# First modulation vectors from w_ada blocks as the stationary operand, first tiles transposed between them

## Chip, cores and metric

The kernel runs on one core of one Trainium2 chip. The metric is device time in microseconds (us); of the kernel before, three runs took 2872.82, 2876.39 and 2877.79 us, median 2876.39.

## What is computed

One layer of a diffusion trunk: an HGRN2 mixer (gated linear recurrence, both directions) and a gated ConvFFN over 2048 latent tokens of width 1024, with 256 context tokens as a prefix. The change is in what comes first, the adaLN modulation:

```python
sc_lat, sc_ctx = jax.nn.silu(c), jax.nn.silu(c_ctx)
m_l = (sc_lat @ w_ada[l] + b_ada[l])[:, None, :]
m_c = sc_ctx @ w_ada[l] + b_ada[l]
sh1, sc1, g1, sh2, sc2, g2 = jnp.split(m_l, 6, axis=-1)
csh1, csc1, cg1, csh2, csc2, cg2 = jnp.split(m_c, 6, axis=-1)
hl = modulate(rmsnorm(lat, norm_g[l, 0]), sh1, sc1)
hc = modulate(rmsnorm(cx, norm_g[l, 0]), csh1, csc1)
```

`modulate(h, shift, scale)` is `h * (1 + scale) + shift`. w_ada is 1024 x 6144 in float32; the first 2048 of its columns give the shift and the scale of the mixer, for two vectors, latent and context.

## The kernel before

Five engines run in order, each through its own list, and wait for each other by semaphores: PE (matrix products), PEld (its loading of the stationary operand, listed apart), DVE (vector), ACT (activation), POOL and SP (which issues most DMAs). A framework orders each list when the program is built, by its own costs and the tiles' buffers.

**The opening** (lines 186 to 253) has four jobs.

*The modulation vectors.* sil (128 x 16) holds SiLU(c) and SiLU(c_ctx) with features on partitions. Line 206 loads w_ada in 16 blocks of 128 x 1024 (512 KB), for k = 0 to 7 and i = 0, 1: i = 0 is the shift, issued on ACT's queue, i = 1 the scale, on SP's. The blocks go through 13 buffers with the tag "wada". Line 209 multiplies with the two columns of sil as the stationary operand and 512 columns of w_ada as the moving one, 32 products into four PSUM tiles mps (2 x 512). Line 216 copies them to SBUF with ACT (m, in two buffers of the pool rawp, tag "raw"), line 220 transposes them in 16 pieces into mt (128 x 16 x 2), and lines 223 to 225 make B1 (shift) and A1 (scale) from mt on DVE, with features on partitions.

*The first three tiles.* early_x loads a tile of 128 tokens and normalizes it: squares on ACT (L100), the inverse root on DVE and POOL (L76, L77), the product on DVE (L105). Tiles 0 to 2 (two of context, one latent; staged[0..2]) come while w_ada arrives, tiles 3 to 6 after. transpose_mod then transposes four blocks of a tile into a PSUM tile tp (L112) and writes scale times tp plus shift to hm, with ACT (L116) or DVE (L119) by turns.

*Splits.* put_split and load_w split a float32 tile into two float32r parts: ACT copies (L80: hh, wh, vh), DVE subtracts (L81: hl, wl, vl). load_feat(0) does this with the first three weight blocks of head 0, load_vg(0) with two more; their raw tiles share the "wada" buffers. load_vg is held behind the instruction ada_done.

*The way on.* The first unit of the mixer (mm3, lines 350 to 352) multiplies hh and hl with wh and wl into z: three products for each of eight blocks k. Its first twelve need hm's blocks k = 0 to 3 of all three tiles, the next twelve k = 4 to 7. Then F (L382 on ACT, L384 on DVE) starts the chain of the recurrence.

The lines that the steps of the prediction touch: w_ada's products L209 (L219 after), transposes L220 (gone after) and L112, scale and shift L223 to L225 (L231 to L233 after), hm L116 and L119 (L124 and L127 after), splits L80 and L81, squares L100.

Of the kernel before, what the change touches and what calls it, by code (L numbers as in the profile page):

```python
# [9 lines left out]
F32 = mybir.dt.float32  # L10
# [3 lines left out]
AF = mybir.ActivationFunctionType  # L14
# [9 lines left out]
KT = 8  # L24
# [24 lines left out]
def body(ctx, tc, a, out):  # L49
    nc = tc.nc  # L50
    pe, act, dve, pool, sp = nc.tensor, nc.scalar, nc.vector, nc.gpsimd, nc.sync
# [11 lines left out]
    ident = cst.tile([128, 128], F32, name="ident")  # L63
# [4 lines left out]
    def small(name, shape=(128, 8), dt=F32):  # L68
        return cst.tile(list(shape), dt, name=name)
# [16 lines left out]
    A1 = [small(f"A1_{i}") for i in range(2)]  # L86
    B1 = [small(f"B1_{i}") for i in range(2)]
    sil = small("sil", (128, 16))
    decb = small("decb", (128, NH, NT))
    def pool_(stack, name, bufs=1, **kw):  # L90
        return stack.enter_context(tc.tile_pool(name=name, bufs=bufs, reuse_waits="tile", **kw))
# [4 lines left out]
    def normalize(xt, junk, stp, on_act=False):  # L96

        ss = stp.tile([128, 1], F32, name="ss", tag="ss", bufs=2)
        rs = stp.tile([128, 1], F32, name="rs", tag="rs", bufs=2)
        act.activation(junk, xt, AF.Square, accum_out=ss)  # L100
        rms_scale(rs, ss, 1, D)
        if on_act:
            act.activation(xt, xt, AF.Copy, scale=rs)
        else:
            dve.tensor_scalar(xt, xt, rs, None, OP.mult)  # L105

    def transpose_mod(xt, hm, g, psp, A, B, tag, bufs, on_act):

        tp = psp.tile([128, 4, 128], F32, name="tp", tag=tag, bufs=bufs)
        for j in range(4):  # L110
            k = g * 4 + j
            pe.transpose(tp[:, j, :], xt[:, k * 128:(k + 1) * 128], ident)  # L112
        for j in range(4):
            k = g * 4 + j
            if on_act:
                act.activation(hm[:, k, :], tp[:, j, :], AF.Identity, bias=B[:, k:k + 1],  # L116
                               scale=A[:, k:k + 1])
            else:
                dve.tensor_scalar(hm[:, k, :], tp[:, j, :], A[:, k:k + 1], B[:, k:k + 1],  # L119
                                  OP.mult, OP.add)  # L120

    ch = ctx.enter_context(ExitStack())
    rawp = pool_(ch, "rawp", 2)
# [15 lines left out]
    def place(i, shape, dt, name):  # L139
        return (hq if i == 5 else hp).tile(shape, dt, name=name, tag=f"place{i}", bufs=1)  # L140
# [7 lines left out]
    def x_tile(p, t, bufs=1, xt=None):  # L148
        if xt is None:
            xt = p.tile([128, D], F32, name="xt", tag="xt", bufs=bufs)  # L150
        src, r = (a["x"], t) if t >= 0 else (a["ctx"], t + 2)
        sp.dma_start(xt, src[r * 128:(r + 1) * 128])
        return xt

    def put_split(hm, u, i, ks=slice(None)):

        c = slice(i * 128, (i + 1) * 128)
        split(part("h", u)[:, ks, c], part("l", u)[:, ks, c], hm[:, ks])

    def load_w(h, ty, wh, wl, p=rawp, tag="raw", bufs=2):  # L160
        raw = p.tile([128, D], F32, name="raw", tag=tag, bufs=bufs)
        sp.dma_start(raw, a["w_in"][h, ty])
        split(wh, wl, raw.rearrange("p (k n) -> p k n", k=KT))

    def load_feat(h, **kw):


        feat = []
        for ty in (2, 1):
            wh = wp.tile([128, KT, 128], F32R, name="wh", tag="wh")  # L170
            wl = wp.tile([128, KT, 128], F32R, name="wl", tag="wl")
            load_w(h, ty, wh, wl, **kw)
            feat.append((wh, wl))
        vh = wp.tile([128, KT, 384], F32R, name="vh", tag="vh", bufs=1)
        vl = wp.tile([128, KT, 384], F32R, name="vl", tag="vl", bufs=1)
        load_w(h, 0, vh[:, :, 256:], vl[:, :, 256:], **kw)
        return feat, vh, vl

    def load_vg(h, w, **kw):

        for i in range(2):
            c = slice(i * 128, (i + 1) * 128)
            load_w(h, 3 + i, w[1][:, :, c], w[2][:, :, c], **kw)


    with ExitStack() as c0:
        p0 = pool_(c0, "p0", side="right")
        p0s = pool_(c0, "p0s", space=PSUM)
        act.activation(sil, vec[:, V_C:V_C + 16], AF.Sigmoid)
        dve.tensor_tensor(sil, sil, vec[:, V_C:V_C + 16], OP.mult)  # L190
        silv = sil.rearrange("p (two k) -> p k two", two=2)
        mps = [p0s.tile([2, 512], F32, name=f"mps{n}") for n in range(4)]
        staged = [v[:, i] for p, n in ((2, 3), (5, 3), (4, 1))
                  for v in [place(p, [128, n, D], F32, "x0")] for i in range(n)]

        def early_x(j):

            xt = x_tile(None, first[j], xt=staged[j])
            junk = p0.tile([128, D], F32, name="junk", tag="hm", bufs=3)
            normalize(xt, junk, p0)  # L200

        first = [t for u in GROUPS[0] for t in u]
        for k in range(KT):
            for i in range(2):
                wt = p0.tile([128, D], F32, name="wada", tag="wada", bufs=13)
                (sp if i else act).dma_start(
                    wt, a["w_ada"][k * 128:(k + 1) * 128, i * D:(i + 1) * D])
                for n in range(2):
                    pe.matmul(mps[2 * i + n], silv[:, k, :], wt[:, n * 512:(n + 1) * 512],  # L209
                              start=k == 0, stop=k == KT - 1)  # L210
            if 3 <= k < 6:
                early_x(k - 3)
        head0 = load_feat(0, p=p0, tag="wada", bufs=13)
        m2 = [rawp.tile([2, 2, 512], F32, name="m2", tag="raw") for _ in range(2)]
        for n in range(4):
            ada_done = act.activation(m2[n // 2][:, n % 2], mps[n], AF.Copy)
        m2f = [m.rearrange("p a b -> p (a b)") for m in m2]
        mt = p0s.tile([128, 16, 2], F32, name="mt")
        for j in range(16):  # L219
            pe.transpose(mt[:, j, :], m2f[j // 8][:, j % 8 * 128:(j % 8 + 1) * 128],  # L220
                         ident[0:2, 0:2])
        for i in (1, 0):
            dve.tensor_tensor(B1[i], mt[:, 0:8, i], vec[:, V_BA:V_BA + 8], OP.add)  # L223
            dve.tensor_tensor(A1[i], mt[:, 8:16, i], vec[:, V_BA + 8:V_BA + 16], OP.add)
            dve.scalar_tensor_tensor(A1[i], A1[i], 1.0, vec[:, V_NG:V_NG + 8], OP.add, OP.mult)  # L225
        hms = [p0.tile([128, KT, 128], F32, name="hm", tag="hm", bufs=3) for _ in range(3)]
        for g in range(2):
            ks = slice(g * 4, g * 4 + 4)
            for j, hm in enumerate(hms):
                m = 0 if first[j] >= 0 else 1  # L230
                transpose_mod(staged[j], hm, g, p0s, A1[m], B1[m], "tr", 3, (g + j) % 2)  # L231
                put_split(hm, 0, j, ks)
        with tc.issue_after(ada_done.ins):  # L233
            load_vg(0, head0, p=p0, tag="wada", bufs=13)
        for j in range(3, 7):
            early_x(j)


        l0, l1 = vec[:, V_LB:V_LB + 16], vec[:, V_LB + 16:V_LB + 32]
        mx = p0.tile([128, 16], F32, name="mx")  # L240
        e2 = p0.tile([128, 2, 16], F32, name="e2")
        eb = p0.tile([128, 32], F32, name="eb")
        pool.memset(eb, float(np.e))
        dve.tensor_tensor(mx, l0, l1, OP.max)
        dve.tensor_tensor(e2[:, 0], l0, mx, OP.subtract)
        dve.tensor_tensor(e2[:, 1], l1, mx, OP.subtract)
        e2f = e2.rearrange("p a b -> p (a b)")
        pool.tensor_tensor(e2f, eb, e2f, OP.pow)
        dve.tensor_tensor(mx, e2[:, 0], e2[:, 1], OP.add)
        dve.reciprocal(mx, mx)  # L250
        dve.tensor_tensor(lb, e2[:, 0], mx, OP.mult)
        dve.tensor_tensor(oml, e2[:, 1], mx, OP.mult)
# [902 lines left out]
    g2, fg, b = [gt[:, k] for k in range(3)]  # L1155
# [247 lines left out]
```

## Time and profile before

| | before |
|---|---|
| median of three runs | 2876.39 us |
| the profiled execution | 2878.25 us |
| its span, first to last instruction | 2876.5 us |
| PE busy | 2812.5 us (98%) |
| DVE, ACT, POOL busy | 2109.9, 1170.6, 587.6 us |
| mean granted clock of TensorE | 0.992 |
| w_ada's products L209, 64 passes | 29.8 us |

A float32 product is two passes on PE, each with a load of the stationary operand of its own, so that 32 products are 64 MATMUL and 64 LDWEIGHTS. A product in float32r, or a transposing one, is one pass. In a row of the trace, the first number is the start in us from the start of the span, the second the time to the end of the last instruction of the row; what stands in brackets is the engine's idle time before and what ended it. Matmuls overlap, so their spacing is read from the starts.

### The profile page before, as it was taken

To read this page: it belongs to the slowest core of one execution; us is meant where nothing else is said; L and a number is where in the kernel's file an instruction comes from. 1 tells how busy PE (TensorE), PEld (TensorE's weight loads), DVE (VectorE), ACT (ScalarE), POOL (GpSimd) and SP (SyncE) were. 2 spreads that over 40 slices of the span, in tenths; PEclk is the share of its full clock that TensorE was granted. 3 is DMA by queue.
4 is the path that set the end of the run, shared out by engine and by line. 5 is a ranking of instruction groups with operands and counts; after the bars stand their busy time and mean duration, and the time that the engine had idled before them with its cause. 6 is when DMAs were issued, how large, how long until landed. Compare 5 with 4: busy or idle time off the path is not lost.

```text
span 2876.5 us, 43715 instructions
## 1 busy us (share of the span) xinstructions
PE 2812.5 (98%) x16016; PEld 2508.9 (87%) x16016; DVE 2109.9 (73%) x3675; ACT 1170.6 (41%) x2500; POOL 587.6 (20%) x1028
## 2 busy tenths in 40 slices
PE   8999999999999999998999799999999999999999
PEld 4999999998999999997888588888888888887887
DVE  5666666667666566577887598888888887677887
ACT  4433333355333333333455444444444444433343
POOL 2111111111111111111111343443444432000001
PEclk9999999999999999999999899999999999999999
DMA  5122222222232222234777622224522224887663
GB/s 229 62 78 84 75 81 85 78 71 97 87 93 62 78 81 79 66 95 163 265 295 281 260 95 84 78 88 161 216 85 73 81 88 130 289 289 254 195 204 121
DMA packets 202911, 386.56 MB, mean 134 GB/s; under 512 B 26692, under 2 KB 117828, under 8 KB 197448
## 3 DMA queue, kind: packets, MB, share of 16 engines
q1 hardware_dynamic: 199960, 375.51, 39.0%
q10 hardware_dynamic: 2736, 8.26, 0.7%
q8 instruction: 126, 2.06, 0.3%
q14 instruction: 89, 0.73, 0.1%
HBM read 281.70 MB, written 101.99 MB: 133 GB/s over the span
## 4 chain that ended last, share of the span: by engine, by line
PE 85%; DMA 6%; DVE 5%; ACT 2%; issue 1%; POOL 1%; SPq 0%; DVEq 0%; POOLq 0%; ACTq 0%
PE z L351 10%; PE z L352 10%; PE z L350 10%; PE zd L712 3%; PE zc L712 3%; PE zc L715 3%; PE zd L715 3%; PE zc L714 3%; PE zd L714 3%; PE za L712 3%; PE za L715 3%; PE za L714 3%; PE y L1237 2%; PE y L1235 2%; PE y L1236 2%; PE kv L554 2%
## 5 line engine op out<-in xcount | busy, mean ns | idle before, releaser
L350 PE MATMUL z<-vh,hh 128*128 128x256 f32 (+1 forms) x1024 | 300.0, 293 | 0.0
L352 PE MATMUL z<-vh,hl 128*128 128x256 f32 (+1 forms) x1024 | 293.5, 287 | 0.0
L351 PE MATMUL z<-vl,hh 128*128 128x256 f32 (+1 forms) x1024 | 293.4, 287 | 0.0
L350 PE MATMUL z<-hh,wh 128*128 128x384 f32 x768 | 263.9, 344 | 3.5 <-ACT hh L80 3.5
L351 PE MATMUL z<-hl,wh 128*128 128x384 f32 x768 | 259.8, 338 | 1.5 <-DVE hl L81 0.9
L352 PE MATMUL z<-hh,wl 128*128 128x384 f32 x768 | 259.6, 338 | 0.0
L1237 PE MATMUL y<-wd,ml 128*128 128x512 f32 x600 | 234.1, 390 | 2.7 <-DVE ml L81 2.7
L1235 PE MATMUL y<-wd,mh 128*128 128x512 f32 x600 | 233.8, 390 | 1.3 <-DVE P L1289 0.7
L1236 PE MATMUL y<-wd,mh 128*128 128x512 f32 x600 | 233.5, 389 | 0.0
L350 PEld LDWEIGHTS z<-vh,hh 128*128 128x128 f32 x1024 | 196.3, 192 | 0.0
L351 PEld LDWEIGHTS z<-vl,hh 128*128 128x128 f32 x1024 | 196.1, 192 | 0.0
L352 PEld LDWEIGHTS z<-vh,hl 128*128 128x128 f32 x1024 | 195.8, 191 | 0.0
L81 DVE TENSOR_TENSOR w<-s,w 128x512 fp32r<-128x512 f32 x132 | 145.6, 1110 | 62.1 <-ACT w L80 62.1
L464 POOL COPY TX<-S 128x3 f32<-128x3 f32 x48 | 15.9, 331 | 772.8 <-DVE S L428 772.8
L80 ACT ACTIVATE w<-raw 128x512 fp32r<-128x512 f32 x176 | 108.8, 626 | 111.7 <-DMA raw<-in_w_up_dram 43.9
L350 PEld LDWEIGHTS z<-hh,wh 128*128 128x128 f32 x768 | 145.5, 190 | 7.9 <-ACT hh L80 4.5
L81 DVE TENSOR_TENSOR w<-raw,w 128x512 fp32r<-128x512 f32 x176 | 122.4, 698 | 40.8 <-ACT w L80 40.4
L404 DVE TENSOR_TENSOR st<-z,st 128x128 f32<-128x128 f32 x127 | 36.4, 287 | 157.8 <-ACT st L403 157.8
L999 DVE SCALAR_TENSOR_TENSOR r<-uv,conv,r 128x1023 f32<-128x1023 f32 (+1 forms) x88 | 149.3, 1715 | 0.4
L351 PEld LDWEIGHTS z<-hl,wh 128*128 128x128 f32 x768 | 145.9, 190 | 2.4 <-DVE hl L81 2.4
L399 ACT ACTIVATE v<-z 128x128 f32<-128x128 f32 x128 | 35.4, 277 | 275.2 <-PE z L352 275.0
L352 PEld LDWEIGHTS z<-hh,wl 128*128 128x128 f32 x768 | 145.6, 190 | 0.0
(325 smaller groups left out, 8158.3 us busy)
## 6 DMA issues: line engine op xcount, KB each, us to landing
raw<-in_w_up_dram SPq DMA_DIRECT2D x90, 512.0 KB, 3.8
raw<-in_w_in_dram SPq DMA_DIRECT2D x80, 512.0 KB, 3.8
lr<-m SPq DMA_DIRECT2D x49, 512.0 KB, 5.4
m<-r SPq DMA_DIRECT2D x66, 256.0 KB, 4.5
raw<-in_w_ada_dram SPq DMA_DIRECT2D x32, 512.0 KB, 4.7
stash<-st SPq DMA_DIRECT2D x125, 128.0 KB, 1.9
kq<-stash SPq DMA_DIRECT2D x15, 1024.0 KB, 7.6
og<-stash SPq DMA_DIRECT2D x15, 1024.0 KB, 6.8
```

Of the source, the lines that this page charges most:

```text
L80: act.activation(h, src, AF.Copy)
L81: dve.tensor_tensor(l, src, h.bitcast(F32), OP.subtract)
L350: pe.matmul(o, sh[:, k], mh[:, k], start=k == 0, stop=False)
L351: pe.matmul(o, sh[:, k], ml[:, k], start=False, stop=False)
L352: pe.matmul(o, sl[:, k], mh[:, k], start=False, stop=k == KT - 1)
L712: pe.matmul(o, w[:, 0, k], r[:, :, 0, k], start=start and k == 0, stop=False, skip_group_check=True)
L714: pe.matmul(o, w[:, 0, k], r[:, :, 1, k], start=False, stop=False, skip_group_check=True)
L715: pe.matmul(o, w[:, 1, k], r[:, :, 0, k], start=False, stop=k == 3, skip_group_check=True)
L999: dve.scalar_tensor_tensor(r, x, cw, r, OP.mult, OP.add)
L1235: pe.matmul(z, lh, rh, start=start, stop=False, skip_group_check=True)
L1236: pe.matmul(z, lh, rl, start=False, stop=False, skip_group_check=True)
L1237: pe.matmul(z, ll, rh, start=False, stop=stop, skip_group_check=True)
```

## The change

w_ada's blocks become the stationary operand: for each of the 16 blocks, eight products take 128 x 128 of it as stationary and the two columns of sil as moving operand, and add up in mt, which DVE sets to zero at the start. That is 128 products, with the features on partitions at once; the four PSUM tiles mps, the copies of L216 and the transposes of L220 go. transpose_mod is cut in two, transpose4 and modulate; the six tiles tp of tiles 0 to 2 (24 transposes) are issued after k = 6 and k = 7 in the code, into six PSUM buffers in place of three.

```diff
-    def transpose_mod(xt, hm, g, psp, A, B, tag, bufs, on_act):
+    def transpose4(xt, g, psp, tag, bufs):
 
         tp = psp.tile([128, 4, 128], F32, name="tp", tag=tag, bufs=bufs)
         for j in range(4):
             k = g * 4 + j
             pe.transpose(tp[:, j, :], xt[:, k * 128:(k + 1) * 128], ident)
+        return tp
+
+    def transpose_mod(xt, hm, g, psp, A, B, tag, bufs, on_act):
+
+        modulate(transpose4(xt, g, psp, tag, bufs), hm, g, A, B, on_act)
+
+    def modulate(tp, hm, g, A, B, on_act):
+
...
-        mps = [p0s.tile([2, 512], F32, name=f"mps{n}") for n in range(4)]
+        mt = p0s.tile([128, 16, 2], F32, name="mt")
+        dve.memset(mt, 0.0)
+        tps = {}
...
-                for n in range(2):
-                    pe.matmul(mps[2 * i + n], silv[:, k, :], wt[:, n * 512:(n + 1) * 512],
-                              start=k == 0, stop=k == KT - 1)
+                for j in range(KT):
+                    ada_done = pe.matmul(mt[:, i * KT + j], wt[:, j * 128:(j + 1) * 128],
+                                         silv[:, k], start=False, stop=k == KT - 1,
+                                         skip_group_check=True)
             if 3 <= k < 6:
                 early_x(k - 3)
+            if k >= KT - 2:
+
+                for j in ((0, 1), (2,))[k - KT + 2]:
+                    for g in range(2):
+                        tps[g, j] = transpose4(staged[j], g, p0s, "tr", 6)
         head0 = load_feat(0, p=p0, tag="wada", bufs=13)
-        m2 = [rawp.tile([2, 2, 512], F32, name="m2", tag="raw") for _ in range(2)]
-        for n in range(4):
-            ada_done = act.activation(m2[n // 2][:, n % 2], mps[n], AF.Copy)
-        m2f = [m.rearrange("p a b -> p (a b)") for m in m2]
-        mt = p0s.tile([128, 16, 2], F32, name="mt")
-        for j in range(16):
-            pe.transpose(mt[:, j, :], m2f[j // 8][:, j % 8 * 128:(j % 8 + 1) * 128],
-                         ident[0:2, 0:2])
...
-                transpose_mod(staged[j], hm, g, p0s, A1[m], B1[m], "tr", 3, (g + j) % 2)
+                modulate(tps[g, j], hm, g, A1[m], B1[m], (g + j) % 2)
```

The order changes with it. On PE, from the end of w_ada's products to the first z of the mixer, before:

```order
L209 MATMUL mps_139<-wada,sil 2x512
L220 MATMUL mt<-ident,m_249 128x2 x8
L220 MATMUL mt<-ident,m_250 128x2 x4
L112 MATMUL tp<-ident,x_140 128x128 x5
L220 MATMUL mt<-ident,m_250 128x2 x4
L112 MATMUL tp<-ident,x_140 128x128 x19
L350 MATMUL z<-hh_290,wh 128x384
```

and from PE's first instruction to that z, of the change (a count here is of products; each of L219 is two passes):

```order
L219 MATMUL mt<-sil,wada 128x2 x64
L112 MATMUL tp<-ident,x_138 128x128 x8
L219 MATMUL mt<-sil,wada 128x2 x24
L112 MATMUL tp<-ident,x_138 128x128 x6
L219 MATMUL mt<-sil,wada 128x2 x8
L112 MATMUL tp<-ident,x_138 128x128 x2
L219 MATMUL mt<-sil,wada 128x2 x24
L112 MATMUL tp<-ident,x_138 128x128 x8
L219 MATMUL mt<-sil,wada 128x2 x8
L358 MATMUL z<-hh_386,wh 128x384
```

All 24 transposes to tp now stand among w_ada's products, and nothing of PE stands between the last of these and z. On ACT, behind the third square of the opening, before:

```order
L100 ACTIVATE junk,ss<-x_140 128x1024
L80 ACTIVATE wh<-raw 128x1024 x2
L80 ACTIVATE vh<-raw 128x8x128
L216 ACTIVATE m_249<-mps_136 2x512
L216 ACTIVATE m_249<-mps_137 2x512
L216 ACTIVATE m_250<-mps_138 2x512
L216 ACTIVATE m_250<-mps_139 2x512
L80 ACTIVATE vh<-raw 128x8x128
L116 ACTIVATE hm<-tp,B_1_108,A_1_106 128x128 x4
```

and at the same place of the change:

```order
L100 ACTIVATE junk,ss<-x_138 128x1024
L124 ACTIVATE hm<-tp,B_1_108,A_1_106 128x128 x3
L80 ACTIVATE wh<-raw 128x1024
L80 ACTIVATE hh_386<-hm 128x4x128
L80 ACTIVATE wh<-raw 128x1024
L124 ACTIVATE hm<-tp,B_1_108,A_1_106 128x128 x2
L80 ACTIVATE vh<-raw 128x8x128
L80 ACTIVATE hh_386<-hm 128x4x128
```

The splits of head 0's weights, of which before three stood ahead of the copies of mps and one behind them, now all stand behind the first hm, which reads A1 and B1; the squares of tiles 3 to 6 come behind the last hh. On DVE, behind the third tile's product L105, before:

```order
L81 TENSOR_TENSOR wl<-raw,wh 128x1024 x2
L81 TENSOR_TENSOR vl<-raw,vh 128x8x128
L223 TENSOR_TENSOR B_1_108<-mt,vec 128x8
L224 TENSOR_TENSOR A_1_106<-mt,vec 128x8
L223 TENSOR_TENSOR B_0_107<-mt,vec 128x8
```

and of the change:

```order
L231 TENSOR_TENSOR B_1_108<-mt,vec 128x8
L232 TENSOR_TENSOR A_1_106<-mt,vec 128x8
L231 TENSOR_TENSOR B_0_107<-mt,vec 128x8
L233 SCALAR_TENSOR_TENSOR A_1_106<-A_1_106,vec 128x8
L232 TENSOR_TENSOR A_0_105<-mt,vec 128x8
L127 TENSOR_SCALAR hm<-tp,A_1_106,B_1_108 128x128
L233 SCALAR_TENSOR_TENSOR A_0_105<-A_0_105,vec 128x8
L127 TENSOR_SCALAR hm<-tp,A_1_106,B_1_108 128x128 x3
L127 TENSOR_SCALAR hm<-tp,A_0_105,B_0_107 128x128 x2
L81 TENSOR_TENSOR wl<-raw,wh 128x1024
```

The three subtractions wl, wl, vl move from ahead of B1 and A1 to behind them. SP's list has the same transfers in the same order; the two loads of head 1's weights no longer wait for m's buffers. From the first F on, every engine has the same instructions in the same order as before, but for some transposes of tiles 3 to 5 that stand a few places earlier or later among the first z.

## The prediction

> **What bounds the kernel now.** First the page, to see which engine sets the time.
>
> ```profile
> span 2876.5 us, 43715 instructions
> ...
> PE 2812.5 (98%) x16016; PEld 2508.9 (87%) x16016; DVE 2109.9 (73%) x3675; ACT 1170.6 (41%) x2500; POOL 587.6 (20%) x1028
> ...
> PE 85%; DMA 6%; DVE 5%; ACT 2%; issue 1%; POOL 1%; SPq 0%; DVEq 0%; POOLq 0%; ACTq 0%
> ```
>
> PE is busy for 98% of the span and is 85% of the chain that ended last. All that the change touches lies in the first 60 us, and from the first F on the lists are the same. So I take it that the opening's end moves the kernel's end by as much, and ask only how much later or earlier the first unit gets its operands. The chain of waits, cut to the first 60 us, says what the opening consists of (start, length, what).
>
> ```profile
> 0.80 3.83 DMA wada<-in_w_ada_dram
> 4.77 29.80 PE mps L209 x64
> 34.57 0.83 PE mt L220 x12
> 35.40 0.69 PE tp L112 x5
> 36.09 0.35 PE mt L220 x4
> 37.02 1.51 ACT hm L116 x4
> ```
>
> PE multiplies w_ada without a pause from 4.77 to 34.57 us; then mt takes until 36.43, and hm begins. Is that PE's own speed, or the transfers'? The timeline of SP and ACT:
>
> ```profile
> 20.23 4.99 SPq L162 DMA_DIRECT2D raw<-in_w_in_dram  x5
> ...
> 35.22 1.61 SPq L162 DMA_DIRECT2D raw<-in_w_in_dram  x2
> ...
> 29.31 1.06 ACT L80 ACTIVATE wh<-raw 128x1024 fp32r<-128x1024 f32 x1 [3.90 <-DMA raw<-in_w_in_dram]
> ```
>
> SP issues the weights of head 0 behind w_ada's last block, and the first has landed at 29.31. I conclude that all of w_ada is there by about 29.3, some 5 us ahead of PE. PE is the bound, and the transfers leave at most 5 us to win.
>
> **The change, part by part.** *128 products in place of 32.* PE's price changes its kind: 512 moving columns give way to a load of 128 stationary columns with two moving ones, 256 passes in place of 64. No row has such a pass. The nearest rows:
>
> ```profile
> 34.50 0.90 PE L220 MATMUL mt<-ident,m 2*128 2x2 f32 x12
> ...
> 41.98 0.44 PE L351 MATMUL z<-hl,wh 128*128 128x384 f32 x1 [0.46 <-DVE hl L81]
> 42.26 0.34 PE L352 MATMUL z<-hh,wl 128*128 128x384 f32 x1
> 42.43 0.34 PE L350 MATMUL z<-hh,wh 128*128 128x384 f32 x1
> 42.61 0.33 PE L351 MATMUL z<-hl,wh 128*128 128x384 f32 x1
> ```
>
> From below: mt also loads 128 columns and moves two, but transposes. Twelve starts lie within 0.90 us less about 0.20 of the last one's own length (the row below), so 0.064 us apart. From above: in z, the first product after a pause comes 0.28 us ahead of the next, the others 0.17 to 0.18. The difference, 0.11, is a non-transposing load that nothing hides. In the changed pass nothing hides it either, since two columns stream in no time: I take 0.115 a pass at full clock (0.11 to 0.12), nearer to z, because z's load does not transpose and w_ada's doesn't either.
>
> ```profile
> L220 PE MATMUL mt<-ident,m x16: 195/196/218, 34.5 to 36.2; 2*128 2x2 f32 x16
> ```
>
> *The clock.* Loads of mps, in PEld's timeline:
>
> ```profile
> 5.58 0.13 PEld L209 LDWEIGHTS mps<-wada,sil 128*2 128x2 f32 x1 [0.73 <-issue]
> 6.43 0.13 PEld L209 LDWEIGHTS mps<-wada,sil 128*2 128x2 f32 x1 [0.73 <-issue]
> ...
> 9.95 0.09 PEld L209 LDWEIGHTS mps<-wada,sil 128*2 128x2 f32 x1 [0.34 <-issue]
> 10.38 0.09 PEld L209 LDWEIGHTS mps<-wada,sil 128*2 128x2 f32 x1 [0.34 <-issue]
> ```
>
> They are 0.85 us apart at first and 0.43 after 9.5: PE starts at half speed and doubles after some 4.5 us of work. The table by stretches (us; busy time and count of PE, PEld, DVE, ACT, POOL; clock; DMA) shows what keeps it up.
>
> ```profile
> core 0: us, PE busy (x) PEld busy (x) DVE busy (x) ACT busy (x) POOL busy (x), PEclk, DMA share, GB/s
> 9.20:34.50 25.30, 25.30 (x59) 4.85 (x58) 9.03 (x14) 8.05 (x12) 8.02 (x27) 1.00 1.03 410
> 43.30:46.70 3.40, 1.09 (x6) 0.72 (x5) 3.37 (x4) 3.40 (x8) 0.00 (x0) 1.00 0.01 5
> 46.70:50.10 3.40, 2.81 (x9) 2.55 (x9) 2.51 (x7) 2.94 (x6) 1.40 (x3) 0.50 0.00 0
> 1343.80:1347.20 3.40, 2.86 (x14) 2.56 (x13) 3.14 (x9) 0.60 (x1) 0.00 (x0) 0.50 0.97 404
> 1347.20:1350.60 3.40, 1.80 (x14) 1.64 (x14) 2.40 (x7) 0.60 (x1) 1.17 (x1) 1.00 0.55 159
> ```
>
> A stretch with PE busy for 1.09 of 3.40 us costs the clock; 2.81 us does not bring it back, 2.86 us does. What counts as busy is open. The row of w_ada itself keeps the full clock with almost no loads (4.85 of 25.30 us) and with two stationary columns of 128, so streaming of the moving operand is enough by itself. In the changed pass streaming is nearly nothing: 512 columns take 0.43 us, hence two take 0.002 of 0.115, 2%. No row shows a stretch filled by loads alone. I choose that only streaming counts: the clock then stays at half during all of the modulation. Half clock doubles a pass: 0.225 us, bounds 0.21 to 0.24.
>
> The Trainium skill, page "TensorE: Matmul & The Clock Gate", section "Part 1: The HAM clock gate (the "warmup" mystery)", has the gate opened by how busy PE has been, after about 3.4 us of sustained activity. The trace agrees for streamed work (doubled after some 4.5 us). By that rule, with loads taken as activity, PE would be at full clock from about 9 us; this is rival A.
>
> *The transposes.* 24 of them move among the products. At half clock:
>
> ```profile
> 51.24 1.05 PE L112 MATMUL tp<-ident,x 128*128 128x128 f32 x4
> ```
>
> Less the last one's 0.42, three spacings of 0.21: 24 cost 5.0 us. The tiles they read are normalized by about 27 us, so they wait for nothing.
>
> *Sum to the first hm.* 4.77 + 256 x 0.225 (57.6) + 24 x 0.21 (5.0) = 67.4 us. The 16 transposes of L220, with the copies, are gone. From mt's end to hm I keep the 0.51 us of before (36.43 to the row below): 67.9.
>
> ```profile
> 36.94 0.41 DVE L119 TENSOR_SCALAR hm<-tp,A,B 128x128 f32<-128x128 f32 x1
> ...
> 52.85 0.47 DVE L384 TENSOR_SCALAR F<-F,oml,lb 128x384 f32<-128x384 f32 x1
> ```
>
> hm begins 31.0 us later than before. The buffers of w_ada are freed later too: the last raw of head 0 waits for w_ada's ninth block, at about 4.8 + 9 x 3.6 = 37 us, with tiles 3 to 6 behind it on SP; their transfers took about 10 us before, so all lands by some 50 us, under the products' cover.
>
> *The splits behind hm.* Of head 0's splits these ran in the shadow of PE's products:
>
> ```profile
> 30.39 2.51 DVE L81 TENSOR_TENSOR wl<-raw,wh 128x1024 fp32r<-128x1024 f32 x2 [3.34 <-ACT wh L80]
> 32.96 1.23 DVE L81 TENSOR_TENSOR vl<-raw,vh 128x1024 fp32r<-128x1024 f32 x1
> ```
>
> In the change ACT waits for A1 and B1 at hm, with wh, wh, vh queued behind it, and DVE's three behind those. They are now paid between the first hm and the first F: 3 x 1.15 us on DVE, which runs nearly without a break there (36.94 to 52.85). I add 3.5 us; bounds 0 (hidden in DVE's waits) and 4.3 (hh also delayed, and the squares of tiles 3 to 6, which now come last).
>
> *Total.* 31.0 + 3.5 = 34.5 us later: 2878.25 + 34.5 = 2912.8 by the profiled execution's own time, which is 1.86 over the median; on the median, 2876.39 + 34.5 = 2910.9. With the bounds of pass (53.8 to 61.4 us) and splits: 2903 to 2916.
>
> **The rivals.** *A, loads count as activity.* Half clock to about 9.2 us as before, 4.4 / 0.225 = 20 passes; then 236 x 0.115 = 27.1, 24 transposes at 0.11 = 2.6, and 0.5: hm at 39.4, 2.5 us late. PE's products cost as much as before, and the transposes, which before came after mt, lengthen them. With the splits 6.0 us: 2882.4. For it: PE is never idle. Against it: no row with loads alone.
>
> *B, a load rides as fast as mt's.* This is the case that ends not slower. At 0.064 us a pass, w_ada needs 16.4 us and PE keeps up with the transfers; hm follows the last block's landing (29.3) by 16 passes, 1.0, and 0.5: 30.8, 6.1 early. The splits give back 3.5: 2873.8, or 2870.3 if they are hidden. It decides from about 0.10 us a pass downwards, where PE stops being later than before. For it: the same 128 columns with two moving. Against it: z's 0.11 for a load that doesn't transpose.
>
> *C, the clock goes up and down*, since the eight transposes in a row stream: 2885 to 2903.
>
> That the transposes are not done early is no rival here: the order shows them among the products. But they stand on the engine that is the bound, so it is no gain until PE waits for blocks.
>
> **How the numbers follow.** Half clock 0.58, A 0.27, B 0.09, C 0.06. The time is the likeliest one's, 2911. The range holds the likeliest, C, and A from 2880 up, about 0.83 in all: 2880 to 2916. Nothing under about 0.2% (5.75 us) can be told from no change in this kernel, so "same" is 2870.6 to 2882.1: most of B (0.06) and nearly half of A (0.11), 0.17. Faster is B's lower edge, 0.03. Slower is the rest, 0.80.
>
> **What would show it.** Spacing of L219's passes: 0.225 us with the clock at 0.50 from the start to about 67 us (half clock), 0.115 with 1.00 from 9 us (A), 0.064 or waits for w_ada's transfers (B). The first hm at 68, 39 or 31 us. The first DVE F some 19.4 us behind the first hm, in place of 15.9. After F, the same distances as before. The forecast is wrong if PE waits for blocks, or if later stages swallow the shift, which would show as idle time of PE that shrinks after 60 us.

## The result and the profile after

| | before | after |
|---|---|---|
| median | 2877.09 us (2872.82 to 2877.89, 4 runs) | 2909.07 us (2903.60 to 2912.72, 4 runs) |
| ratio | 1 | 1.0111 (95% interval 1.0095 to 1.0127) |
| profiled execution: time, span | 2878.25, 2876.5 us | 2912.72, 2911.0 us |
| first hm on VectorE | 36.94 us | 64.85 us |
| first F on VectorE | 52.85 us | 84.71 us |

The change costs 32.0 us, 1.1%; the forecast was 2911. The profiled execution is the slowest of the four, so it shows 34.4 us. The chain of waits of the kernel after, cut to the opening (start, length, what):

```profile
4.89 27.44 PE mt L219 x128
32.33 1.81 PE tp L112 x8
34.14 10.03 PE mt L219 x48
44.17 1.38 PE tp L112 x6
45.55 3.21 PE mt L219 x16
48.76 0.53 PE tp L112 x2
49.29 10.03 PE mt L219 x48
59.32 1.81 PE tp L112 x8
61.13 3.22 PE mt L219 x16
64.37 0.17 DVE B L231
```

From 4.89 to 64.35 us nothing is in it but TensorE. Divide 10.03 by 48, or 27.44 by 128: about 0.21 us a pass, from the first to the last (the starts in the trace are 0.2133 us apart). At no point does the spacing of the passes change, so at no point did the clock. The clock column can't be used for this here: the trace has no clock record of this kernel before 79.9 us, and a stretch without one is shown as 1.00. The spacing is what the reader has to go by.

Behind the last product, VectorE and ScalarE in the kernel after (timelines, one fence each):

```profile
64.85 0.41 DVE L127 TENSOR_SCALAR hm<-tp,A,B 128x128 f32<-128x128 f32 x1
...
67.04 1.23 DVE L81 TENSOR_TENSOR wl<-raw,wh 128x1024 fp32r<-128x1024 f32 x1
...
68.78 1.22 DVE L81 TENSOR_TENSOR wl<-raw,wh 128x1024 fp32r<-128x1024 f32 x1
70.14 1.23 DVE L81 TENSOR_TENSOR vl<-raw,vh 128x1024 fp32r<-128x1024 f32 x1
...
84.71 0.47 DVE L392 TENSOR_SCALAR F<-F,oml,lb 128x384 f32<-128x384 f32 x1
```

```profile
64.91 1.16 ACT L124 ACTIVATE hm<-tp,B,A 128x128 f32<-128x128 f32 x3 [38.09 <-DVE A L232]
65.95 1.06 ACT L80 ACTIVATE wh<-raw 128x1024 fp32r<-128x1024 f32 x1
```

ScalarE stands idle for 38.09 us until A is there, with wh queued behind hm; before, wl, wl and vl were done by 34.2 us. From hm to F it now takes 19.86 us instead of 15.91, and VectorE is busy there for 16.73 us instead of 13.26: 3.5 us more, the three subtractions.

Where the 34.4 us of the two profiled executions come from: first hm 27.9 later, first F 31.9 later. Behind F, I compared each instruction of VectorE with the one that has the same place from the end of the list in the kernel before: 31.2 us later at 149 us of before's time, 31.4 at 1232, 33.9 at 1357, 34.5 at the end. Most of the step lies where one phase of the kernel gives way to the next. The table by stretches there, of before and, 31 us later, of after (us; busy time and count of PE, PEld, DVE, ACT, POOL; clock; DMA):

```profile
1334.00:1369.00 35.00, 26.44 (x141) 21.60 (x142) 25.45 (x73) 8.84 (x22) 4.25 (x4) 0.90 0.67 232
```

```profile
1365.00:1400.00 35.00, 26.00 (x124) 21.45 (x123) 21.96 (x64) 8.37 (x22) 3.55 (x3) 0.76 0.60 202
```

TensorE is idle for about the same time in both (8.6 and 9.0 us), and the clock is at half for 6.8 us before and for 17.1 us after (mean 0.90 and 0.76).

### The profile page after: what moved, and what is told of

Its sections match the earlier page's. It is cut to its first block, busy times and chain, and to the rows that moved or that the text cites. A ratio compares the mean times of both kernels' runs of the same rounds, so it can differ in the third digit from the quotient of the medians.

```text
span 2911.0 us, 44065 instructions
## 1 busy us (share of the span) xinstructions
PE 2841.6 (98%) x16192; PEld 2564.3 (88%) x16192; DVE 2120.3 (73%) x3676; ACT 1168.5 (40%) x2496; POOL 588.7 (20%) x1028
## 4 chain that ended last, share of the span: by engine, by line
PE 90%; DVE 3%; DMA 2%; ACT 2%; issue 1%; POOL 1%; SPq 0%; DVEq 0%; POOLq 0%; ACTq 0%
PE z L360 10%; PE z L359 10%; PE z L358 10%; PE y L1245 4%; PE y L1243 4%; PE y L1244 4%; PE zd L720 3%; PE zc L720 3%; PE zc L722 3%; PE zd L722 3%; PE zd L723 3%; PE zc L723 3%; PE za L720 3%; PE za L722 3%; PE za L723 3%; PE y L804 2%
## 5 line engine op out<-in xcount | busy, mean ns | idle before, releaser
L81 DVE TENSOR_TENSOR w<-raw,w 128x512 fp32r<-128x512 f32 x176 | 132.2, 754 | 40.2 <-ACT w L80 39.6
L358 PEld LDWEIGHTS z<-hh,wh 128*128 128x128 f32 x768 | 145.6, 190 | 13.6 <-ACT hh L80 10.1
```

What stands on the lines that cost most here:

```text
L81: dve.tensor_tensor(l, src, h.bitcast(F32), OP.subtract)
L358: pe.matmul(o, sh[:, k], mh[:, k], start=k == 0, stop=False)
```

## The experiments

The theory on trial: the passes are slow because the clock is at half, the clock is at half because only streamed moving columns keep it up, and the splits cost the rest. Rivals: loads count, and something else held the clock; a load costs 0.2133 us at any clock; the half clock under the first z costs what I gave to the splits. All landmarks at a glance (first hm and F on VectorE in the profiled execution; one run each but for before, after and the three with column groups):

| kernel | pass of the new form | first hm | first F | hm to F | time |
|---|---|---|---|---|---|
| before | | 36.94 | 52.85 | 15.91 | 2877.1 |
| after | 0.213 | 64.85 | 84.71 | 19.86 | 2909.1 |
| streamed beside | 0.213, then 0.112 | 77.45 | 92.31 | 14.86 | 2912.5 |
| shift streamed | 0.112 | 39.90 | 55.65 | 15.75 | 2881.2 |
| streamed start | 0.112, then 0.213 | 65.40 | 85.25 | 19.85 | 2912.7 |
| a third streamed | 0.112, 0.213, 0.112 | 84.64 | 99.31 | 14.67 | 2923.8 |
| splits first | 0.213 | 64.98 | 80.69 | 15.71 | 2903.1 |
| products alone | 0.213 | 60.71 | 81.40 | 20.69 | 2906.0 |
| transposes alone | | 38.37 | 54.26 | 15.89 | 2881.7 |
| column groups | | 31.20 | 49.88 | 18.67 | 2875.1 |
| column groups, transposes early | | 31.51 | 50.27 | 18.75 | 2875.3 |
| column groups, x first | | 31.43 | 52.60 | 21.17 | 2876.0 |

### Streamed products beside the new ones

```
+        for _ in range(5):
+            pe.matmul(fz, ident[:, 0:2], ft, start=True, stop=True)
...
+                for n in range(2):
+                    pe.matmul(fz, silv[:, k, :], wt[:, n * 512:(n + 1) * 512], ...)
```

> The kernel after, with work added and no result changed: five products of 512 moving columns that need no w_ada run ahead of the stage, and beside the 8 new products (16 passes) of each w_ada block stand the 2 products of 512 moving columns of the kernel before, into a PSUM tile that nobody reads. Theory (only streamed moving columns count as activity, so the new stage stays at half clock, and a pass costs 0.2133 us only because of that): the clock rises during the first products and stays up, the passes of the new products stand 0.105 to 0.115 us apart, a block takes 1.71 + 1.71 = about 3.4 us, as long as in the kernel after although it does twice the work; 16 blocks are 55 us behind a start of 5 to 12 us, the first hm lies at 62 to 69 us, the total at 2905 to 2915. Rival 1 (a load with so few columns behind it takes 0.2133 us whatever the clock): a block takes 3.41 + 1.71 = 5.1 us, hm at about 93 us, total about 2937. Rival 2 (nothing brings the clock up before about 80 us in these kernels): both parts at half clock, 6.8 us a block, hm at about 118 us, total about 2962. On the distance from the first hm to the first F: 19.9 us as in the kernel after if the splits of the weights behind A1 and B1 cost the extra 4 us, about 16 us if it was the half clock under the first z products.

The chain of this kernel (L224 new products, L207 the five ahead, L228 the old form beside each block):

```profile
4.85 13.82 PE mt L224 x64
18.66 7.28 PE fz L207 x10
25.94 6.87 PE fz L228 x16
32.80 1.88 PE mt L224 x16
34.68 1.81 PE fz L228 x4
```

The five products were issued behind four blocks of new ones, not ahead of them, so my numbers for the first hm (62 to 69 us, measured 77.5) miss. It made the test a better one. The same 16 passes take 13.82 / 4 = 3.46 us while nothing has been streamed, and 1.88 us behind 14 us of streaming, in which the clock came up (the streamed passes stand 0.85 us apart at first and 0.43 from 24.5 us on). Inside a block they stand 0.2133 and 0.112 us apart. Rival 1, a load that costs the same at any clock, is out; so is the idea that nothing brings the clock up here. What also shows: at full clock the new form of a block costs 1.88 us and the old one 1.81. They were never different in price.

### Shift blocks in the old form

```
+                if i == 0:
+                    for n in range(2):
+                        pe.matmul(fz, silv[:, k, :], wt[:, n * 512:(n + 1) * 512], ...)
+                    continue
```

> The kernel after, with the blocks of the shift half of w_ada multiplied in the old form (2 products of 512 moving columns, into a PSUM tile that nobody reads, so the shift is b_ada alone in this kernel and its product is left out of the output), and the blocks of the scale half in the new form; the two take turns, and nothing runs ahead of them. Theory (only streamed columns count, and the share needed to raise the clock is higher than the one to keep it): half of each stretch of 6.8 us is streamed at most, which does not raise the clock: every block of either form takes 3.41 us, the new passes stand 0.213 apart, hm at 62 to 66 us, total as the kernel after, 2903 to 2913. Rival 1 (loads count too, but something else held the clock down): full clock by about 10 us, 1.71 us a block, the stage bounded by the transfers that end near 29 us, hm at 33 to 40 us, total 2874 to 2884. Rival 2 (a share of one half is enough to raise it, late): blocks of 1.71 us from some point on, hm between 40 and 60 us.

```profile
4.91 3.57 PE fz L221 x4
8.48 2.21 PE mt L225 x16
10.69 1.81 PE fz L221 x4
12.49 1.88 PE mt L225 x16
```

This kernel leaves the shift's product out of its output. What I had expected of my own theory fell: the clock rose within the second block (2.21 us) and stayed, the first hm came at 39.9 us, 2881.2 us in all. Those are the numbers of rival 1, loads that count. But my expectation had overlooked that the first block alone streams for 3.57 us, so the clock can rise on it; from then on half of the time is streamed, which keeps it. This kernel alone can't tell the two apart. The next one does.

### Streaming at the start only

```
+                if (k, i) == (0, 0):
+                    for n in (0, 1, 0, 1):
+                        pe.matmul(fz, silv[:, k, :], wt[:, n * 512:(n + 1) * 512], ...)
```

> The kernel after with one addition: block 0 of w_ada is first multiplied twice in the old form (4 products, 8 passes of 512 moving columns, into a PSUM tile that nobody reads); all 16 blocks then follow in the new form. Theory (the clock follows the streamed columns alone, up and down): the 8 passes bring the clock up by about 9 us, the new passes behind them start at 0.117 us, and with nothing streamed beside them the clock falls again within two or three stretches of 3.4 us, after which they stand 0.213 apart as in the kernel after: first hm at 66 to 71 us (5 us of added work, about 3 us of gain), total 2909 to 2918. Rival (new passes hold a clock that is up, and only could not raise it): 256 passes at 0.117 us and 24 transposes at 0.113 us, first hm at 41 to 45 us, total 2881 to 2889.

Here the trace has clock records from 7.7 us on. Table by stretches:

```profile
core 0: us, PE busy (x) PEld busy (x) DVE busy (x) ACT busy (x) POOL busy (x), PEclk, DMA share, GB/s
...
9.87:14.40 4.53, 4.53 (x42) 4.53 (x42) 1.49 (x6) 1.15 (x2) 4.53 (x17) 1.00 1.02 408
14.60:32.90 18.30, 18.30 (x88) 18.30 (x88) 3.26 (x5) 2.30 (x4) 2.93 (x10) 0.50 0.99 393
32.99:61.60 28.61, 28.61 (x138) 28.61 (x138) 0.00 (x0) 0.00 (x0) 0.00 (x0) 0.50 0.39 148
```

TensorE and its loads are busy for all of every stretch, and wait for nothing. Eight streamed passes brought the clock up, the first new passes stand 0.112 us apart, and at 14.5 us the clock is gone and stays at 0.50 until 79.4 us: back-to-back loads with two moving columns each neither raise the clock nor keep it. This is the run that settles the choice on which the forecast stood, and the rival that loads hold a clock which is up (41 to 45 us) is out with it. The first hm, 65.40 us, lies a little below my 66 to 71: until 14.5 us the passes won back most of the 4.9 us of added work.

### One third streamed

The kernel above, with one product of the old form kept beside each later block too.

> The kernel after with one product of the old form (2 passes of 512 moving columns, into a PSUM tile that nobody reads) beside each w_ada block, four beside the first. At full clock a block is 0.90 us streamed and 1.88 us of new passes, a share of one third against one half in the kernel with both products beside each block, which kept the clock. Theory (a share between one third and one half is needed to keep it; stretches at half clock elsewhere in these traces point at somewhat under 0.4): the clock comes up by 9 us and is lost again within the stage, then blocks of 2.6 times 2 = 5.2 us, or it goes up and down; first hm at 65 to 95 us. Rival (any streaming holds it): 16 blocks of 2.8 us and 2.7 us of transposes, first hm at 54 to 59 us, total 2893 to 2901.

```profile
10.88:19.80 8.92, 8.92 (x60) 6.28 (x59) 4.09 (x8) 2.30 (x4) 6.25 (x23) 1.00 1.02 409
20.00:75.20 55.20, 55.20 (x192) 37.96 (x192) 5.81 (x6) 6.43 (x7) 0.54 (x1) 0.50 0.45 167
75.20:77.90 2.70, 2.70 (x14) 2.70 (x15) 0.00 (x0) 0.00 (x0) 0.00 (x0) 0.50 0.00 0
78.00:84.00 6.00, 6.00 (x42) 4.09 (x40) 0.00 (x0) 0.00 (x0) 0.00 (x0) 1.00 0.00 0
```

A share of 0.95 of 2.83 us streamed lost the clock at 19.9 us; about one half (1.81 of 3.69 us) kept it with the shift blocks streamed. So in these kernels the limit lies between 0.34 and 0.49. Streaming too little is the worst of all, 2923.8 us, since the added products are paid at half clock too.

### The splits first

```
+        after_act, after_dve = [ins.ins for ins in last_split]
+        with tc.issue_after(after_dve):
             for i in (1, 0):
                 dve.tensor_tensor(B1[i], mt[:, 0:8, i], vec[:, V_BA:V_BA + 8], OP.add)
...
+                with tc.issue_after(after_act):
                     modulate(tps[g, j], hm, g, A1[m], B1[m], (g + j) % 2)
```

> The kernel after, with the two wh splits and the vh and vl, wl splits of the first weights issued ahead of A1, B1 and the first hm on ScalarE and VectorE; TensorE's order is untouched. Theory (the splits behind A1 and B1 cost what the kernel after lost between the first hm and the first F): first hm unchanged at 64.4 to 65.0 us, F 15.9 to 16.8 us behind it instead of 19.9, all later work 3 to 4 us earlier than in the kernel after up to 1200 us, total 2902 to 2909. Rival (the half clock under the first z products, which lasts until 79.9 us in the kernel after, is what stretches that part): F moves by less than 1.5 us, total 2907 to 2912.

ScalarE's and VectorE's timelines:

```profile
30.36 1.06 ACT L80 ACTIVATE wh<-raw 128x1024 fp32r<-128x1024 f32 x1 [5.06 <-DMA raw<-in_w_in_dram]
31.64 1.06 ACT L80 ACTIVATE wh<-raw 128x1024 fp32r<-128x1024 f32 x1 [0.22 <-DMA raw<-in_w_in_dram]
32.91 1.06 ACT L80 ACTIVATE vh<-raw 128x1024 fp32r<-128x1024 f32 x1 [0.21 <-DMA raw<-in_w_in_dram]
34.16 1.06 ACT L80 ACTIVATE vh<-raw 128x1024 fp32r<-128x1024 f32 x1 [0.19 <-DMA raw<-in_w_in_dram]
65.04 1.86 ACT L124 ACTIVATE hm<-tp,B,A 128x128 f32<-128x128 f32 x5 [29.82 <-DVE A L236]
```

```profile
80.69 0.48 DVE L397 TENSOR_SCALAR F<-F,oml,lb 128x384 f32<-128x384 f32 x1
```

The weights landed between 30 and 34 us. With the splits back under the products, hm to F takes 15.71 us, 4.15 less than in the kernel after, with TensorE's order as it was and its first z again 0.32 us apart, at half clock. The table's column agrees in every kernel: 14.7 to 15.9 where the splits come first (in five of these six with the first z 0.32 us apart, as in the kernel after), 18.7 to 20.7 where they come behind hm, and 21.2 where the x tiles go first as well. The rival, z's half clock, is out. All later work is 27.4 us behind the kernel before up to 560 us, as against 31.2.

### One part of the change at a time

Products alone: all 24 transposes issued behind the last product.

```
-            if k >= KT - 2:
-                for j in ((0, 1), (2,))[k - KT + 2]: ...
+                with tc.issue_after(ada_done.ins):
+                    tp = transpose4(staged[j], g, p0s, "tr", 6)
```

> The kernel after with the second part of the change undone: the new products stay, and all 24 transposes of the first three x tiles are issued behind the last of them. Theory (the early transposes lengthen TensorE's chain at half clock, and cost what they take there, about 5.3 us, since TensorE waits for nothing in this stage): the last pass ends at 4.9 + 256 x 0.2133 = 59.5 us, the first hm waits for 4 transposes, 60.4 to 61.2 us, and F lies 19.9 to 21 us behind it, at 80.3 to 82 us instead of 84.7; all later work 26.5 to 29 us behind the kernel before, total 2902 to 2908. Rival (behind the products they delay the hm by as much, so that their place is worth nothing): hm at 60.4 to 61.2 us, but F at 84 us or later and the total as in the kernel after, 2903 to 2913.

```profile
4.94 54.77 PE L219 MATMUL mt<-sil,wada 128*128 128x2 f32 x256 [4.94 <-DVE sil L198]
59.58 4.84 PE L112 MATMUL tp<-ident,x 128*128 128x128 f32 x24
```

All 256 passes stand in one row: 4.94 to 59.58, 0.2133 us each. The first hm comes 4.1 us earlier than in the kernel after and F 3.3 us earlier: the early transposes lengthen TensorE's chain, which has no wait to put them in. But little of that lasts, and there my theory (26.5 to 29 us behind the kernel before) missed: from 149 to 560 us all later work is 30.4 us behind, only 0.8 less than in the kernel after. Between F and there it loses the clock once more often than the kernel after, from 101.3 to 108.1 us. The single run, 2906.0 us, lies among the four of the kernel after (2903.60 to 2912.72). So the early transposes are no gain; that they cost more than 0.8 us beyond the opening isn't shown.

Transposes alone: before's products, with 12 of the transposes (as many as the three buffers of tp hold) among the last blocks.

> The kernel before with one part of the change alone: its products and its order of the splits stay, and 12 of the 24 transposes of the first three x tiles (the first half of each tile) stand among the last w_ada blocks on TensorE. Theory (this part neither costs nor brings more than its own time): the stage of w_ada ends 1.3 us later, the first hm no longer waits for its transposes, first hm within 1.5 us of the 36.9 of the kernel before, total within 3 us of 2877. Rival (early transposes lower the clock under the last blocks, as passes without streamed columns do): half clock appears before 46 us, hm 2 to 4 us later, total 2880 or more. Rival 2 (they were the whole gain of the change, hidden by its loss): hm at 34 us or earlier, total 2874 or less.

```profile
4.92 26.73 PE mps L218 x56
31.64 1.02 PE tp L112 x8
32.67 3.52 PE mps L218 x8
36.19 0.59 PE tp L112 x4
36.78 1.09 PE mt L232 x16
```

Here the early transposes run at full clock: 1.02 + 0.59 us more on TensorE, first hm 1.4 us later (38.37), all later work 1.1 us behind up to 560 us. It took 2881.7 us, 4.2 over the kernel before, a little more than the 3 I had allowed; by the trace 2.5 of that come behind 1232 us. Half clock did appear before 46 us, as the rival had said, from 40.8 us where the kernel before has it from 46.7. But the last blocks kept the full clock (0.43 us a pass): it fell behind a pause of TensorE (37.9 to 40.0 us), ahead of the first z, and hm was not 2 to 4 us late.

### Column groups: does the stage follow the transfers once TensorE is out of the way?

```
+                    r = 32 * (2 * i + n)
+                    pe.matmul(mps[r:r + 2], silv[:, k, :], wt[:, n * 512:(n + 1) * 512],
+                              start=False, stop=k == KT - 1, skip_group_check=True)
...
+        ada_done = act.activation(m2, mps, AF.Copy)
+        for j in range(4):
+            pe.transpose(mt[:, j].rearrange("p a b -> p (a b)"), m2[:, j * 128:(j + 1) * 128], ident)
```

> The kernel before with its products in the old form, but the four sums of 512 columns in one PSUM bank at output partitions 0, 32, 64 and 96 (zeroed by VectorE, all products adding), so that the four products of one k use different column groups of the array; behind them one copy of 128x512 by ScalarE and 4 transposes in place of 4 copies and 16 transposes. Theory (products in different column groups run side by side, and TensorE was the bound of this stage in the kernel before): TensorE keeps up with w_ada, whose transfers end near 29.3 us, first hm at 31 to 33 us instead of 36.9; the splits of the weights, which land at 30 to 34 us, then stand between hm and F, so of the 4 to 5 us some 2 to 5 are left: total 2871 to 2876. Rival (the groups take turns): a pass 0.45 us as before, first hm at 36 to 37 us, total 2875 to 2879. Rival 2 (side by side, the share of streaming falls and with it the clock): passes twice as long without harm, first hm at 32 to 34 us, transposes and first z products at half clock, total 2873 to 2879.

The chain of the opening, and TensorE's waits for its products:

```profile
4.14 10.90 DMA wada<-in_w_ada_dram
15.12 11.47 DMA wada<-in_w_ada_dram
26.63 1.16 PE mps L211 x8
27.79 0.59 PE tp L112 x4
28.38 0.98 PE mps L211 x4
```

```profile
  DMA wada<-in_w_ada_dram: 25.9, 16
```

Passes now start in pairs 0.007 us apart. TensorE waits 16 times for w_ada, and transfers have taken its place in the chain. The first hm comes at 31.20 us, 5.7 earlier: 5.2 because the last pass ends at 29.36 us and not at 34.57, the other 0.5 lies behind it, where one copy and 4 transposes stand in place of 4 and 16. From hm to F it takes 18.67 us, which gives 2.8 of it back. Most of the splits now stand behind hm, and VectorE is busy for 16.6 us of that stretch, 3.3 more than in the kernel before. The clock did fall, as rival 2 had it (transposes 0.21 us apart from 33.8 us, first z 0.32); the kernel with the splits first speaks against a cost of that, but no run with column groups tells the two apart. Median 2875.13 us (10 runs) beside 2877.55: ratio 0.9990, interval 0.9979 to 1.0001.

> The kernel with four column groups, and as in the change all 24 transposes of the first three x tiles stand among the last two w_ada blocks. Theory: the transposes (24 at 0.11 to 0.22 us, 2.7 to 5.3 us) fit into TensorE's waits for w_ada if the column groups run side by side; first hm as in the kernel with column groups alone, F up to 2 us earlier than there, total 2869 to 2875. Rival (groups take turns, so TensorE is the bound and the transposes lengthen it, as the transposes alone did with 1.1 us for 12): first hm at 39 us, total 2877 to 2882.

With all transposes early as well: first hm 31.51, F 50.27 us, 2875.29 us, ratio 0.9993 (0.9983 to 1.0003). TensorE has waits to put them in, and still F is not up to 2 us earlier, as theory had it. By the chain of waits ScalarE and VectorE set the time from hm to F: they are busy for 15.9 and 16.6 of its 18.8 us, TensorE for 10.1.

> The kernel with four column groups, and the next four x tiles fetched and normalised ahead of the second pair of weights (v and g) instead of behind it, to take the wait of F behind the last normalisations on VectorE away (1.4 us of idle time for GpSimd and 0.75 us a tile in the kernel with column groups alone). Theory: first hm unchanged at 31 to 31.6 us, F at 47.5 to 49.5 us instead of 49.9, total 2868 to 2874 and below the kernel before by 0.1 to 0.3%. Rival (ScalarE and VectorE are full between hm and F whatever the order): F at 49.5 to 51 us, total as with column groups alone, 2873 to 2877.

Fetching and normalising the next four x tiles earlier made F later, against theory and rival: 52.60 us. The squares and normalisations went ahead of hh and hl, for which z now waits. TensorE's timeline:

```profile
42.01 0.67 PE L352 MATMUL z<-hh,wh 128*128 128x384 f32 x1
45.55 0.69 PE L353 MATMUL z<-hl,wh 128*128 128x384 f32 x1 [2.87 <-DVE hl L81]
```

Its median was 2876.00 us, ratio 0.9998 (0.9989 to 1.0007).

> The kernel with four column groups once more, beside the one with the x tiles fetched first, for its interval: its first F lay 3.0 us earlier than in the kernel before, its time 2.4 us lower with an interval from 6.0 us lower to 0.3 us higher. Theory (it is faster by its 3 us): ratio 0.9985 to 0.9995, interval below 1. Rival (no difference): interval from below 1 to above 1.

2874.05 us (11 runs) beside 2876.37, ratio 0.9992, interval 0.9983 to 1.0001. Its profiled execution had the first hm at 32.60 and F at 51.26 us, a gain of 4.3 and 1.6. Twice 2.3 to 2.4 us lower in the median, and twice with an interval that just takes in 1: the column groups beat the kernel after by some 34 us, but that they beat the kernel before isn't shown.

## Why the prediction was right, step by step

1. **TensorE bounds the stage, the transfers end near 29 us.** Right. With column groups the last block is multiplied by 29.4 us.
2. **A pass at full clock 0.115 us.** Right: 0.112, 1.88 us for a block's 16. Rival B's 0.064 (mt's row) is out. Why mt's passes are faster isn't shown: they transpose, but they also load from 2 partitions and not 128. The Trainium skill, page "TensorE: Matmul & The Clock Gate", section "LDWEIGHTS (loading the stationary operand)", gives a load as its columns divided by 1.2, in ns, 107 for 128; the trace agrees at full clock (0.112 us a pass) and has twice that at half (0.2133).
3. **Only streaming counts, so half clock throughout.** Right, and shown by the kernel that streams at the start only. The Trainium skill, same page, section "Part 1: The HAM clock gate (the "warmup" mystery)", speaks of how busy TensorE is; in that kernel it was busy without a gap and the clock fell, so passes that load 128 columns and move two are no activity in its sense.
4. **0.225 us a pass at half clock, 57.6 us.** Too high: 0.2133, 54.6 us. A half-clock pass is 1.9 of the full-clock ones, 0.2133 by 0.112, and I had taken about twice 0.115. This term is nearly the whole miss at hm: 3.0 of the 3.1 us between 67.9 predicted and 64.85 measured.
5. **24 transposes 5.0 us.** 4.9: the chain's last pass ends at 64.35, and less 4.89 and 54.6 that is what is left for them. Issued late instead, F comes only 3.3 us earlier, and 0.8 of it is left at 149 us.
6. **Splits 3.5 us, bounds 0 to 4.3.** 3.95 measured, of which VectorE's added work is 3.5; 4.15 taken away by the kernel with splits first.
7. **After F the same distances.** Right to 1232 us (31.9 at F, 31.2 to 31.4 later), wrong behind: 34.5 at the end. The half clock at the change of phases lasted 10 us longer. So it is luck that the profiled execution came out as close to the sum as it did (+34.5 forecast, +34.4 measured): 2.6 us too much up to F (steps 4 and 6 together) met 2.6 us behind F that I hadn't foreseen. Between the medians it is +32.0, close to what stood at F.

Rival A had the products of a clock that is up about right: its sum put the first hm at 39.4 us, and with half of the blocks streamed it came at 39.90. That the totals lie so close (2882.4 by its sum, 2881.2 measured) is in part chance, since the sum has 3.5 us for splits that come first in that kernel (hm to F 15.75). Even at full clock the change would not have paid on TensorE, since a block costs 1.88 us in the new form and 1.81 in the old.

What stays open is the late part. Between 149 us and the end the kernels gain or lose against the kernel before, with the same instructions there: 4.9 us gained (streamed beside), 2.6 gained (splits first, products alone), 3.4 lost (streamed start), 3.2 lost (after), 2.4 lost (transposes alone). The time at half clock behind 1300 us is 31.4, 31.0 and 33.4 us in those that gained, 41.5, 47.9 and 38.9 in those that lost, and 32.9 in the kernel before. That would fit the clock's drops as a cause, but products alone gained with a little more half clock than the kernel before, the kernel with a third streamed has 37.0 us of it and lost nothing (0.2 gained), and no experiment moved the drops alone.

## What to carry to other kernels

Before you swap the operands of a product, price both forms on TensorE by what is loaded and what is streamed: 8 products that load 128 columns cost as much here as 2 that stream 512 (1.88 and 1.81 us a block), so nothing could be won, and a stage of such loads alone also lost the clock, which made a pass 0.2133 us in place of 0.112. Work that is put "into the shadow" of an engine that never waits only lengthens it (transposes), and work that another engine did in that shadow may be queued behind the result instead (splits): look at the order on every engine, not at the engine that you change. Where the stage can be made cheaper for TensorE, ask what is next; here 5.7 us won at hm were 3.0 at F, and 2.4 in the median of the runs, which is not clear of noise.

## What the runs showed of the hardware that I had not expected

- The clock rose on 3.57 us of streamed work at the start, and a share of 0.49 streamed kept it from then on; 0.34 lost it after some 10 us, and no streaming at all after 4.7 (9.8 to 14.5 us, streamed start).
- Transposes of 128x128 seem to count as activity: in the kernel with a third streamed, the clock came back at 77.9 us, at the end of a stretch of 2.7 us that held transposes alone (the row 75.20:77.90). With the products alone, too, 54.6 us of new passes left the clock at half, and of the 24 transposes behind them the first 20 stand 0.21 us apart and the last ones, from 63.8 us, 0.11. Eight of them in a row, 1.81 us, did not bring it back in the kernel after.
- Products into PSUM partitions 0 and 32, or 64 and 96, of one bank run side by side: two passes of 512 columns start 0.007 us apart, against 0.43 us in the kernel before.
